# Moving the low parts of weights, rope, recurrence and gated sums from GpSimd to VectorE, and the high parts to ScalarE, in a two-layer hybrid attention block on one core

## Chip, cores and metric

The kernel runs on one core of one Trainium2 chip. The metric is the device time of one execution in microseconds (us), the median of three runs. A core has TensorE (PE in the rows, with its weight loads under PEld), VectorE (DVE), ScalarE (ACT), GpSimd (POOL) and SyncE (SP, which here issues the DMAs).

## The reference

Two layers over 512 latent tokens and 256 context tokens (768 together), model width 1024. Cut to what matters:

```python
for l in range(DEPTH):
    # adaLN: shift, scale and gate from w_mod; h = x * (1 + sc1) + sh1
    px, pc = split_in(h_x @ w_in), split_in(h_c @ w_in)
    y_mla  = attention of 8 heads, 64 + 32 (rope) wide, over ranks 256 and 128
    y_hg   = gated linear recurrence forwards and backwards, 4 heads of 128
             # f = lb + (1 - lb) * sigmoid(z); S = diag(f) S + k v^T; o = S^T q
    y_diff = (softmax(q1 k1) - lam * softmax(q2 k2)) v, 4 heads of 2 x 64, rope, RMS norm
    m  = sum over br of sigmoid(h @ w_gate[br] + b_gate[br]) * (y[br] @ w_branch[br])
    x  = layer_norm(alpha * x + g1 * (m @ w_o))
    x  = layer_norm(alpha * x + g2 * ((silu(gate) * up) @ w_ff2))   # gate, up = h @ w_ff1
```

Latent queries read context and latent tokens, context queries only context ones. All of it is float32.

## The kernel before

Every product is made from split operands: a high part (fp32r) and a low part (raw minus high), and three matmuls, high by high, high by low and low by high (`mm3`). A weight tile is loaded raw by a DMA (`wr`, 128x1024 or 128x512), `split_w` (L352) writes its high part `wh` and its low part `wl`, and both lie in rings of three buffers. `do_conv` (L365) splits tiles up to two jobs ahead of use.

All engines' orders are fixed when the program is built. A planner (`Clock`, L110) keeps a modelled clock for each engine, `self.ck.at[...]`, and every call goes through it. Its helper records every instruction, which is why all rows say L106 and work is told apart by tile names. Names: `h` activations (high and low), `wr`, `wh`, `wl` weights, `S` two score tiles of two PSUM banks each, `b` four single PSUM banks, `k` eight tiles for split heads, `s` slabs in SBUF, `sm` one-column statistics, `ident` the identity (a matmul with it is a transpose), `c` the conditioning vector, `ac` FFN activations, `colv` gate biases.

The program is two streams. One is a list of jobs, each of which uses one weight tile. The other is a generator for what waits on chains of small steps: `mla`, then `diff`, then `hgrn`, then the layer norm. `weave` (L433) puts them together. Where the generator yields `At(t)`, jobs are written until TensorE's modelled clock has reached t; where a job yields `Need(tok)`, the generator has to come that far first. The jobs of a layer come in this order: the projections (`uq_jobs`, `win_jobs`, and those of the modulation, `mod_block`), then `merge_jobs` for the branches 0, 2 and 1 (the first two numbers below are branch and place), then the output projection and the FFN (`sweep_jobs`). In `merge_jobs` a gate job multiplies `h` with a tile of `w_gate` and evacuates with a Sigmoid on ScalarE (`s<-b,colv` in the rows); a branch job multiplies the attention output with a tile of `w_branch`:

```python
                if len(st["y"]) < 4:
                    yield Need(f"y{l}_{br}")
                    yield Need(f"y{l}_2")
...
        lag = (6, 2, 8)[seq]
```

`y{l}_2` is set where `diff` ends. So the first branch job can be written only when `diff` is over; six gate jobs stand before it.

`diff` goes tile by tile (a head by 128 queries, against 768 keys for latent queries, 256 for context). Step by step: score matmuls into both `S` tiles (`sA`), a maximum on VectorE (`sm<-S`), an Exp on ScalarE (`s<-S,sm`), `sm<-sm,nlam,sm` and the difference `s<-s,sm,s` on VectorE (`sB3`), transposes of it (`b<-ident,s`, `S<-ident,s`) and their split into `k` (a cast on ScalarE, `k<-b,k` and `k<-S,k` on VectorE, `sC`), the product with the values (`b<-k,k`), and the norm of the output. In between `prep_qk` prepares the next head: rope, split, and value transposes. `hgrn` takes each head through log2 levels: on each level a copy `s<-k` on ScalarE, a matmul `S<-k,s`, and products of `k` tiles by gates (`k<-k,k`, `k<-k,s`); at L1427 one of them, 128x768, stands on GpSimd, the others on VectorE.

In the profiled execution the stages lie so, in us: start 0 to 120; layer 0: `mla` to 400, `diff` to 715, `hgrn` to 960, the rest of merge to 1080, norm and output projection to 1260, FFN to 1860; layer 1: `mla` to 2100, `diff` to 2275, `hgrn` to 2525, norm to 2660, FFN to 3000.

Of the kernel before, what the change touches and what calls it, by code (L numbers as in the profile page):

```python
# [10 lines left out]
F32 = mybir.dt.float32  # L11
# [221 lines left out]
class Job:  # L233
    def __init__(self, body, load=None, n=0, eng="vector", cost=0.0):
        self.body, self.load, self.n, self.eng, self.cost = body, load, n, eng, cost
        self.raw = self.hi = self.lo = None
        self.defer = self.late = False
        self.conv = None
        self.hold = False


class Kern:
# [647 lines left out]
    def uq_jobs(self, l):  # L890
# [4 lines left out]
        for half in range(2):  # L895
# [10 lines left out]
            def body(job, half=half):  # L906
# [3 lines left out]
                for hh in range(4):  # L910
# [3 lines left out]
                    def evac(ps, o, n):  # L914
                        if o == XO:
# [4 lines left out]
                            nc.gpsimd.tensor_tensor(qs[64:96, o:o + n], qs[64:96, o:o + n], tmp[64:96, :n], ALU.add)  # L920
# [49 lines left out]
    def win_jobs(self, l, names):  # L970
# [3 lines left out]
        for nmj, j in names:  # L974
# [18 lines left out]
            self.add(Job(body, self.load_fm(w, NK), 1024, "gpsimd", 24 * sum(mmcost(g[1]) for g in groups)))  # L993


    def mla(self, l):
# [54 lines left out]
        def sB2(i):  # L1051
# [5 lines left out]
            nc.gpsimd.tensor_scalar(pr[:, :n], pr[:, :n], rs[:], 1.0, ALU.mult, ALU.mult)  # L1057
# [85 lines left out]
    def diff(self, l):  # L1143
# [19 lines left out]
        def prep_qk(h):  # L1163
            rq, rqs, rk, rks, rv = st["raw", h]
            nc.gpsimd.tensor_tensor(rqs[:, XO:], rqs[:, XO:], rope[1][:, :TX], ALU.mult)
            yield
            nc.gpsimd.tensor_tensor(rks[:, XO:], rks[:, XO:], rope[1][:, :TX], ALU.mult)
            yield
            for rr, rs in ((rq, rqs), (rk, rks)):
                nc.vector.tensor_tensor(rr[:, XO:], rr[:, XO:], rope[0][:, :TX], ALU.mult)  # L1170
                nc.vector.tensor_tensor(rr[:, XO:], rr[:, XO:], rs[:, XO:], ALU.add)
                yield
# [14 lines left out]
            for g, m in ((0, 4), (4, 2)):  # L1187
                ps = self.bank()
# [5 lines left out]
                yield  # L1194
# [99 lines left out]
        for _ in prep_qk(0):  # L1294
            yield 1.0
        yield At(ck.ready(*[x[:, :, o0:] for x in st["qk", 0][:2]], st["v", 0]))
        n = len(tiles)
        per = n // 4
        pg = None
        for i in range(n + 3):  # L1300
            if i < n:
# [8 lines left out]
                if pg is not None:  # L1310
                    next(pg, None)
# [3 lines left out]
                if pg is not None:  # L1315
                    next(pg, None)
            elif i == n:
                sB3(i - 1)
            if 1 <= i <= n:
# [5 lines left out]
                if i < n and pg is not None:  # L1325
                    next(pg, None)
# [12 lines left out]
            if i < n and i % per == per - 1 and pg is not None:  # L1339
                for _ in pg:  # L1340
                    pass
# [8 lines left out]
    def hgrn(self, l):  # L1350
# [13 lines left out]
        def gen(h):  # L1364
            r = st.pop(("raw", h))
            KK, QQ, TT = self.k6([P, 2, T]), self.k6([P, 2, T]), self.k6([P, 2, T])
            for d, nmj in enumerate(("ff", "fb")):
                nc.scalar.activation(TT[:, d], r[nmj][:], AF.Sigmoid)
                nc.scalar.activation(KK[:, d], r[nmj][:], AF.Sigmoid, scale=-1.0)
                if l > 0:  # L1370
                    lb, l1 = self.lb[:, d, h:h + 1], self.lb1[:, d, h:h + 1]
                    nc.gpsimd.tensor_scalar(TT[:, d], TT[:, d], l1, lb, ALU.mult, ALU.add)
                    nc.gpsimd.tensor_scalar(KK[:, d], KK[:, d], l1, 1.0, ALU.mult, ALU.mult)
# [4 lines left out]
            nc.gpsimd.tensor_tensor(sq[:, o0:], KK[:, 0, o0:], KK[:, 1, o0:], ALU.add)  # L1378
# [5 lines left out]
            nc.gpsimd.tensor_tensor(g[:, o0:], g[:, o0:], sg[:, o0:], ALU.mult)  # L1384
# [28 lines left out]
            for lv in range(NLEV):  # L1413
# [13 lines left out]
                nc.gpsimd.tensor_tensor(kv, kv, tk, ALU.mult)  # L1427
# [105 lines left out]
    def merge_jobs(self, l, br, seq):  # L1533
# [30 lines left out]
        for o in range(8):  # L1564
# [9 lines left out]
            jg = Job(gate, self.load_fm(I["w_gate"][l, br][:, o * P:(o + 1) * P], NK), 1024, "gpsimd", 24 * sum(mmcost(g[1]) for g in groups))  # L1574
            gates.append(jg)

            def bran(job, o=o):
# [27 lines left out]
            brans.append(Job(bran, self.load_fm(I["w_branch"][l, br][:, o * P:(o + 1) * P], 4), 512, "gpsimd", 12 * sum(mmcost(g[1]) for g in groups)))  # L1605
# [8 lines left out]
    def sweep_jobs(self, key, w, nk, tiles, lhs, use_s, needs=(), keep=2):  # L1614
# [4 lines left out]
        for k in range(nk):  # L1619
# [31 lines left out]
            jb = Job(body, load, 1024, "vector")  # L1651
# [370 lines left out]
```

## Time and profile before

| | us |
|---|---|
| median of 3 runs (3018.76 to 3024.58) | 3023.1 |
| the profiled execution, its own time | 3024.47 |
| its span | 3022.7 |
| TensorE busy | 2764.9 |
| VectorE busy | 1652.6 |
| ScalarE busy | 1159.8 |
| GpSimd busy | 975.8 |

Busy times are sums over the instructions of an engine; engines work side by side, so they don't add up to the span. The span is what the profile covers, and the own time is that of the same execution as the runs are timed. The granted clock is TensorE's clock as the profile shows it, as a share of its full level (2.4 GHz); 0.5 is its lower level (1.2 GHz), and a mean in between is a mix of both.

### The profile page before, as it was taken

Reading aid. Unit: us, or ns where it says so; the run is one execution under the profiler, and the core shown is the slowest. Engines: PE = TensorE matmul, PEld = TensorE weight load, DVE = VectorE, ACT = ScalarE, POOL = GpSimd, SP = SyncE. Lnnn points to the kernel's source line nnn. Section 1 sums busy time; section 2 is a strip of 40 time slices with the busy share of each in tenths; the row PEclk is TensorE's granted clock in tenths of the full one; section 3 lists DMA queues with packets and bytes.
Section 4 is the critical chain, followed back from the end, with each engine's and each line's share of the span. In section 5 each row is a group of like instructions: output and inputs, shape, how many; then the busy total and the mean of one; then the engine's idle time right before and its main releaser. Section 6 shows DMA issues by size and latency. Waiting matters only on the chain. (4 is left out here: it accounts for less than half of the span.)

```text
span 3022.7 us, 39134 instructions
## 1 busy us (share of the span) xinstructions
PE 2764.9 (91%) x14899; PEld 2330.5 (77%) x14899; DVE 1652.6 (55%) x2410; ACT 1159.8 (38%) x2205; POOL 975.8 (32%) x685
## 2 busy tenths in 40 slices
PE   6999988878889998999999989999899899799997
PEld 3888867767778886788888768888787777688875
DVE  4555567667774137555543576455766764622235
ACT  4544435444432223443432355443544432322222
POOL 1343332223444433333320124344334654300002
PEclk8999999999999999999999999999999999899998
DMA  6433253323332444343533254324223444433331
GB/s 214 119 104 95 97 146 112 110 88 110 110 110 88 125 160 160 126 138 113 154 105 126 100 194 116 94 84 136 87 81 102 149 134 131 136 99 98 105 126 70
DMA packets 345523, 359.14 MB, mean 119 GB/s; under 512 B 31114, under 2 KB 263044, under 8 KB 345336
## 3 DMA queue, kind: packets, MB, share of 16 engines
q1 hardware_dynamic: 343144, 351.84, 37.1%
q10 hardware_dynamic: 1680, 4.42, 0.4%
q8 instruction: 117, 1.92, 0.3%
q14 instruction: 70, 0.57, 0.1%
q0 software_dynamic: 512, 0.39, 0.1%
HBM read 298.10 MB, written 58.49 MB: 118 GB/s over the span
## 5 line engine op out<-in xcount | busy, mean ns | idle before, releaser
L106 PE MATMUL b<-h,wh 128*128 128x512 f32 (+1 forms) x5152 | 1374.5, 355 | 35.0 <-ACT h L106 14.7
L106 PEld LDWEIGHTS b<-h,wh 128*128 128x128 f32 x5152 | 908.8, 193 | 164.4 <-ACT h L106 15.8
L106 PE MATMUL b<-h,wl 128*128 128x512 f32 (+1 forms) x2576 | 907.6, 352 | 0.8 <-DVE wl L106 0.8
L106 DVE TENSOR_TENSOR wl<-wr,wh 128x1024 fp32r<-128x1024 f32 (+1 forms) x250 | 357.6, 1433 | 472.1 <-ACT wh L106 469.9
L106 PEld LDWEIGHTS b<-h,wl 128*128 128x128 f32 x2576 | 494.7, 192 | 66.4 <-DVE wl L106 1.6
L106 ACT CAST wh<-wr 128x1024 fp32r<-128x1024 f32 (+1 forms) x304 | 301.0, 994 | 427.4 <-PE b L106 344.3
L106 POOL TENSOR_TENSOR sm<-sm,mhalf 128x1 f32<-128x1 f32 (+3 forms) x80 | 56.8, 711 | 1053.3 <-DVE sm L106 1041.2
L106 POOL TENSOR_TENSOR wl<-wr,wh 128x1024 fp32r<-128x1024 f32 (+1 forms) x134 | 292.1, 2180 | 228.2 <-ACT wh L106 176.6
L106 ACT ACTIVATE s<-S,sm 128x768 f32<-128x768 f32 (+1 forms) x170 | 135.3, 797 | 387.6 <-DVE sm L106 312.4
L106 POOL TENSOR_TENSOR ln<-ln,wr 128x512 f32<-128x512 f32 x84 | 119.5, 1424 | 222.6 <-issue 161.6
L106 PE MATMUL S<-wh,ac 128*128 128x512 f32 x512 | 175.0, 407 | 16.6 <-DVE ac L106 11.5
L106 DVE TENSOR_TENSOR k<-b,k 128x512 fp32r<-128x512 f32 (+1 forms) x136 | 85.3, 628 | 170.0 <-ACT k L106 169.7
L106 PE MATMUL b<-ident,s 128*128 128x128 f32 (+3 forms) x687 | 112.3, 278 | 70.3 <-DVE s L106 24.7
L106 PE MATMUL S<-k,s 128*128 128x128 f32 (+2 forms) x704 | 130.0, 309 | 35.7 <-DVE k L106 33.8
L106 PE MATMUL b<-k,wh 128*128 128x512 f32 (+1 forms) x576 | 160.0, 366 | 1.2 <-ACT wh L106 1.1
L106 DVE TENSOR_REDUCE sm<-S 128x1 f32<-128x768 f32 (+1 forms) x160 | 131.7, 838 | 52.9 <-PE S L106 52.8
L106 PEld LDWEIGHTS b<-ident,s 128*128 128x128 f32 (+3 forms) x687 | 80.3, 143 | 93.0 <-issue 27.7
L106 PE MATMUL S<-k,k 96*128 96x512 f32 (+2 forms) x576 | 136.9, 340 | 12.6 <-DVE k L106 10.4
L106 POOL TENSOR_SCALAR wh<-wr 128x1024 fp32r<-128x1024 f32 (+1 forms) x80 | 82.9, 1039 | 198.6 <-PE b L106 166.3
L106 PEld LDWEIGHTS S<-k,s 128*128 128x128 f32 x704 | 105.4, 203 | 50.0 <-issue 30.7
L106 DVE TENSOR_TENSOR k<-s,k 96x768 fp32r<-96x768 f32 (+7 forms) x92 | 116.3, 1281 | 47.3 <-ACT k L106 44.5
L106 POOL TENSOR_TENSOR s<-s,s 128x512 f32<-128x512 f32 (+2 forms) x88 | 114.3, 1309 | 66.1 <-DVE s L106 43.2
(184 smaller groups left out, 4210.9 us busy)
## 6 DMA issues: line engine op xcount, KB each, us to landing
wr<-in_w_ff_dram SPq DMA_DIRECT2D x154, 512.0 KB
wr<-in_w_mod_dram SPq DMA_DIRECT2D x96, 512.0 KB
d<-s SPq DMA_DIRECT2D x88, 384.0 KB
wr<-in_w_in_dram SPq DMA_DIRECT2D x64, 512.0 KB
s<-d SPq DMA_DIRECT2D x80, 384.0 KB
wr<-in_w_gate_dram SPq DMA_DIRECT2D x48, 512.0 KB
wr<-in_w_branch_dram SPq DMA_DIRECT2D x48, 256.0 KB
wr<-in_w_o_dram SPq DMA_DIRECT2D x24, 512.0 KB
```

Source lines behind the costliest of these rows:

```text
L106: return getattr(getattr(self.clock.nc, self.eng), op)(*a, **k)
```

## The change

GpSimd is taken out of the weight split, of `mla`'s normalisation, of rope, of the recurrence and of the gated sums. The high part of a weight is always written by ScalarE, the low part always by VectorE; the products and sums go to VectorE; two scalings of the gates in layer 1 go to ScalarE. In `diff`, the value transposes now yield an `At` for a free bank and for the loaded values, and the driving loop passes it on (`step`). The planner's choice between engines (`lo_eng`) goes away. GpSimd keeps the layer norm's affine, the modulation's part of it, and the power -0.5.

```diff
-    def split_w(self, hi, lo, raw, eng=None):
+    def split_w(self, hi, lo, raw):
         nc = self.nc
-        if self.kp is not None and not self.inhg and self.ck.at["gpsimd"] + 1.0 < self.ck.at["scalar"]:
-            nc.gpsimd.tensor_scalar(hi, raw, 1.0, 1.0, ALU.mult, ALU.mult)
-        else:
-            nc.scalar.copy(hi, raw)
-        (eng or nc.vector).tensor_tensor(lo, raw, hi.bitcast(F32), ALU.subtract)
-
-    def lo_eng(self, j):
-        if self.inhg and j.eng == "gpsimd" and self.ck.at["vector"] < self.ck.at["gpsimd"] + 1.0:
-            return self.nc.vector
-        return getattr(self.nc, j.eng)
+        nc.scalar.copy(hi, raw)
+        nc.vector.tensor_tensor(lo, raw, hi.bitcast(F32), ALU.subtract)
...
-            self.split_w(j.hi[:, :j.n], j.lo[:, :j.n], j.raw[:, :j.n], self.lo_eng(j))
+            self.split_w(j.hi[:, :j.n], j.lo[:, :j.n], j.raw[:, :j.n])
...
-            nc.gpsimd.tensor_scalar(pr[:, :n], pr[:, :n], rs[:], 1.0, ALU.mult, ALU.mult)
+            nc.vector.tensor_scalar(pr[:, :n], pr[:, :n], rs[:], None, ALU.mult)
...
-            nc.gpsimd.tensor_tensor(rqs[:, XO:], rqs[:, XO:], rope[1][:, :TX], ALU.mult)
-            yield
-            nc.gpsimd.tensor_tensor(rks[:, XO:], rks[:, XO:], rope[1][:, :TX], ALU.mult)
-            yield
             for rr, rs in ((rq, rqs), (rk, rks)):
+                nc.vector.tensor_tensor(rs[:, XO:], rs[:, XO:], rope[1][:, :TX], ALU.mult)
+                yield
...
             for g, m in ((0, 4), (4, 2)):
+                yield At(max(ck.next("b", 4), ck.ready(rv)))
                 ps = self.bank()
...
+        def step(pg):
+            r = next(pg, None) if pg is not None else None
+            if r is not None:
+                yield r
+                next(pg, None)
...
-                if pg is not None:
-                    next(pg, None)
+                yield from step(pg)
...
-                    nc.gpsimd.tensor_scalar(TT[:, d], TT[:, d], l1, lb, ALU.mult, ALU.add)
-                    nc.gpsimd.tensor_scalar(KK[:, d], KK[:, d], l1, 1.0, ALU.mult, ALU.mult)
+                    nc.scalar.activation(TT[:, d], TT[:, d], AF.Identity, scale=l1, bias=lb)
+                    nc.scalar.activation(KK[:, d], KK[:, d], AF.Identity, scale=l1)
...
-                nc.gpsimd.tensor_tensor(kv, kv, tk, ALU.mult)
+                nc.vector.tensor_tensor(kv, kv, tk, ALU.mult)
...
-                        nc.gpsimd.tensor_tensor(sg[:, oo:oo + n], sg[:, oo:oo + n], mo[:, oo:oo + n], ALU.add)
+                        nc.vector.tensor_tensor(sg[:, oo:oo + n], sg[:, oo:oo + n], mo[:, oo:oo + n], ALU.add)
```

Counted over the whole program, GpSimd goes from 690 instructions to 228, VectorE from 2412 to 2778, ScalarE from 1954 to 2074 (24 of these are table loads, which go from 13 to 37); TensorE and SyncE keep their numbers, 14369 and 916. What moves: 96 `wl` of 128x1024 and 38 of 128x512, 70 `wh` of 128x1024 and 10 of 128x512, 80 normalisations of `mla`, 88 rope products, `hgrn` products and gated sums (`s<-s,s`), 56 products of the recurrence, 8 sums `s<-k`, and 16 gate scalings.

Because the planner's clocks set the order, the change also moves instructions that it doesn't name. First, TensorE where layer 0's `diff` ends. Before, the transposes and the product of one of the last tiles are followed by matmuls of a gate job, `b<-h,wh` and `b<-h,wl`:

```order
L106 MATMUL b_6554<-ident,s_6437 128x128 x2
L106 MATMUL b_6559<-ident,s_6502 128x128
L106 MATMUL b_6559<-k_5776,k_6475 128x256 x12
L106 MATMUL b_6546<-h_114,wh_6277 128x256
L106 MATMUL b_6546<-h_115,wh_6277 128x256
L106 MATMUL b_6546<-h_114,wl_6278 128x256
```

After, the last tiles follow one upon the other, and the next row of a job is that of the first branch job, `b<-k,wh`:

```order
L106 MATMUL b_6876<-ident,s_6809 128x128 x2
L106 MATMUL b_6881<-ident,s_6846 128x128
L106 MATMUL b_6881<-k_6199,k_6819 128x256 x12
L106 MATMUL b_6912<-ident,s_6865 128x128 x2
L106 MATMUL b_6917<-ident,s_6896 128x128
L106 MATMUL b_6917<-k_6199,k_6875 128x256 x4
L106 MATMUL b_6933<-ident,s_6924 128x128
L106 MATMUL b_6933<-k_6199,k_6911 128x256 x4
L106 MATMUL b_6949<-ident,s_6940 128x128
L106 MATMUL b_6968<-s_6208,sel 2x512
L106 MATMUL b_6985<-k_6973,wh_6582 128x512 x2
L106 MATMUL b_6985<-k_6973,wl_6583 128x512
```

The last row of a job ahead of them is row 2938 and the next is row 2985: 46 rows (2939 to 2984) of four tiles and the end of two more stand with no job between them, where before gate jobs stand in every such place. In layer 1 the same is so for 23 rows (9657 to 9679), with one tile's scores. The same gate jobs now stand earlier in the program.

Second, ScalarE in the middle of layer 0's `diff`. Before, exps (`s<-S,sm`) of neighbouring tiles, with casts and the norm of the output between them:

```order
L106 ACTIVATE s_5349,sm_5352<-s_5349 128x128
L106 ACTIVATE s_5386,sm_5385<-S_3874,sm_5384 128x768
L106 ACTIVATE s_5395,sm_5394<-S_3875,sm_5393 128x768
L106 CAST wh_5439<-wr_5276 128x1024
L106 CAST k_5450<-b_5451 128x256
L106 ACTIVATE s_5180<-b_5457,subg_500 128x128
L106 ACTIVATE s_5464<-b_5457,sm_5298 128x128
L106 ACTIVATE s_5464,sm_5467<-s_5464 128x128
L106 ACTIVATE s_5485,sm_5484<-S_3874,sm_5483 128x768
L106 ACTIVATE s_5495,sm_5494<-S_3875,sm_5493 128x768
L106 COPY s_5438<-b_5443 128x512
```

After, at the same tiles, Sigmoids of gate jobs (`s<-b,colv`) stand among the exps, and a table load stands at each step from one to the other:

```order
L106 ACT_TABLE_LOAD
L106 ACTIVATE s_5803,sm_5802<-S_4129,sm_5801 128x768
L106 ACTIVATE s_5812,sm_5811<-S_4130,sm_5810 128x768
L106 CAST wh_5817<-wr_5600 128x1024
L106 ACT_TABLE_LOAD
L106 ACTIVATE s_5737<-b_5738,colv 128x512
L106 CAST k_5847<-b_5848 128x256
L106 ACTIVATE s_5589<-b_5854,subg_500 128x128
L106 ACTIVATE s_5861<-b_5854,sm_5699 128x128
L106 ACTIVATE s_5861,sm_5864<-s_5861 128x128
L106 ACT_TABLE_LOAD
L106 ACTIVATE s_5882,sm_5881<-S_4129,sm_5880 128x768
```

Of the 24 added loads 12 stand in layer 0's `diff` and 12 in layer 1's.

Third, the levels of the recurrence in layer 0's `hgrn`. Before, on VectorE:

```order
L106 TENSOR_TENSOR s_6893<-S_6886,ident 128x768
L106 TENSOR_TENSOR s_6895<-k_6808 128x768
L106 TENSOR_TENSOR k_6807<-k_6807,k_6808 128x384 x2
L106 COPY_PREDICATED s_6893<-mask,S_6898 128x768
L106 TENSOR_TENSOR k_6808<-s_6895 128x384
L106 TENSOR_TENSOR k_6807<-k_6807,s_6895 128x192x2 x2
L106 COPY_PREDICATED s_6893<-mask,S_6928 128x768
```

and beside it on GpSimd the wide product of each level:

```order
L106 TENSOR_TENSOR k_6806<-k_6806,k_6808 128x384x2
L106 TENSOR_TENSOR k_6806<-k_6806,s_6895 128x192x2x2
L106 TENSOR_TENSOR k_6806<-k_6806,k_6808 128x96x2x4
L106 TENSOR_TENSOR k_6806<-k_6806,s_6895 128x48x2x8
L106 TENSOR_TENSOR k_6806<-k_6806,k_6808 128x24x2x16
```

After, on VectorE alone:

```order
L106 TENSOR_TENSOR s_7078<-S_7071,ident 128x768
L106 TENSOR_TENSOR k_7022<-k_7022,k_7024 128x384x2
L106 TENSOR_TENSOR s_7080<-k_7024 128x768
L106 TENSOR_TENSOR k_7023<-k_7023,k_7024 128x384 x2
L106 COPY_PREDICATED s_7078<-mask,S_7093 128x768
L106 TENSOR_TENSOR k_7022<-k_7022,s_7080 128x192x2x2
L106 TENSOR_TENSOR k_7024<-s_7080 128x384
L106 TENSOR_TENSOR k_7023<-k_7023,s_7080 128x192x2 x2
```

The wide product `k<-k,k 128x384x2` (`128x192x2x2` on the next level) now stands on VectorE's queue ahead of the level's others.

## Rows read from the trace of the kernel before

**Rows 1.** The page, part 1: busy time and share of each engine.

```profile
PE 2764.9 (91%) x14899; PEld 2330.5 (77%) x14899; DVE 1652.6 (55%) x2410; ACT 1159.8 (38%) x2205; POOL 975.8 (32%) x685
```

**Rows 2.** Windows: stretch, its length, busy us of each engine; granted clock; DMA share.

```profile
120.00:400.00 280.00, 273.54 (x1697) 238.21 (x1696) 148.33 (x277) 127.73 (x282) 111.67 (x91) 1.00 0.40 122
400.00:625.00 225.00, 188.30 (x1069) 157.94 (x1067) 156.45 (x260) 101.92 (x229) 67.08 (x52) 0.92 0.34 106
625.00:715.00 90.00, 75.70 (x424) 64.09 (x425) 53.22 (x88) 52.01 (x105) 28.16 (x21) 0.92 0.35 111
715.00:960.00 245.00, 211.91 (x1337) 186.01 (x1336) 176.40 (x232) 81.02 (x155) 107.43 (x59) 0.95 0.30 101
1860.00:2100.00 240.00, 233.43 (x1412) 205.01 (x1411) 126.81 (x215) 99.70 (x211) 108.16 (x79) 1.00 0.37 111
2100.00:2275.00 175.00, 154.16 (x871) 132.30 (x870) 117.68 (x200) 86.33 (x196) 59.53 (x42) 0.95 0.33 99
2275.00:2525.00 250.00, 229.44 (x1234) 191.54 (x1233) 173.77 (x252) 93.87 (x182) 136.54 (x85) 0.99 0.38 118
2215.00:2275.00 60.00, 56.96 (x333) 49.65 (x332) 33.81 (x73) 31.31 (x74) 22.36 (x16) 0.97 0.31 94
```

**Rows 3.** Timeline, layer 1's diff: start, duration, idle before with its releaser in brackets.

```profile
2206.22 3.24 DVE L106 SCALAR_TENSOR_TENSOR s<-s,sm,s 128x768 f32<-128x768 f32 x1
2206.26 2.38 POOL L106 TENSOR_TENSOR wl<-wr,wh 128x1024 fp32r<-128x1024 f32 x1
...
2209.61 0.63 PE L106 MATMUL b<-ident,s 128*128 128x128 f32 x4 [1.71 <-DVE sm L106]
```

**Rows 4.** Timeline, layer 0's diff, a difference of two tiles with GpSimd still.

```profile
501.79 1.02 DVE L106 SCALAR_TENSOR_TENSOR s<-s,sm,s 128x768 f32<-128x768 f32 x1
```

**Rows 5.** Timeline, layer 0's hgrn, one level of the recurrence.

```profile
773.46 3.03 POOL L106 TENSOR_TENSOR k<-k,k 128x768 f32<-128x768 f32 x1 [1.47 <-ACT s L106]
...
776.52 0.94 ACT L106 COPY s<-k 128x768 f32<-128x768 f32 x1 [3.20 <-POOL k L106]
...
780.37 0.93 PE L106 MATMUL S<-k,s 128*128 128x128 f32 x4 [3.34 <-DVE k L106]
```

**Rows 6.** The page, part 5: groups (busy us, mean ns, idle before and its releaser).

```profile
L106 ACT CAST wh<-wr 128x1024 fp32r<-128x1024 f32 (+1 forms) x304 | 301.0, 994 | 427.4 <-PE b L106 344.3
L106 POOL TENSOR_TENSOR wl<-wr,wh 128x1024 fp32r<-128x1024 f32 (+1 forms) x134 | 292.1, 2180 | 228.2 <-ACT wh L106 176.6
```

**Rows 7.** Groups by form on VectorE, 2700 to 2940, FFN of layer 1.

```profile
L106 DVE TENSOR_TENSOR wl<-wr,wh 128x1024 fp32r<-128x1024 f32 x44 | 53.9, 1226 | 126.5 <-ACT wh L106 126.5
```

**Rows 8.** Groups by form on VectorE, 715 to 960, hgrn of layer 0.

```profile
L106 DVE TENSOR_TENSOR wl<-wr,wh 128x1024 fp32r<-128x1024 f32 x10 | 23.0, 2307 | 0.6 <-ACT wh L106 0.6
```

**Rows 9.** Groups by form on ScalarE, 400 to 715, diff of layer 0.

```profile
L106 ACT ACTIVATE s<-S,sm 128x768 f32<-128x768 f32 x32 | 28.9, 902 | 69.0 <-DVE sm L106 56.8 <-issue 12.0 <-ACT k L106 0.2
...
L106 ACT CAST k<-b 128x512 fp32r<-128x512 f32 x20 | 11.6, 582 | 3.3 <-PE b L106 3.3
...
L106 ACT ACT_TABLE_LOAD x7 | 9.0, 1283 | 0.1
```

**Rows 10.** Groups by form on VectorE, 400 to 715.

```profile
L106 DVE TENSOR_REDUCE sm<-S 128x1 f32<-128x768 f32 x32 | 29.2, 942 | 4.5 <-PE S L106 4.5
...
L106 DVE TENSOR_TENSOR k<-b,k 128x512 fp32r<-128x512 f32 x20 | 13.8, 690 | 22.6 <-ACT k L106 22.5
L106 DVE TENSOR_REDUCE sm<-S 128x1 f32<-128x256 f32 x16 | 6.0, 407 | 0.0
```

**Rows 11.** Timeline of ScalarE, 656 to 660: a table load among exps.

```profile
657.24 1.28 ACT L106 ACT_TABLE_LOAD   x1
658.54 0.69 ACT L106 ACTIVATE s<-b,colv 128x512 f32<-128x512 f32 x1
```

**Rows 12.** Timeline of TensorE, 636 to 682: its first and last waits behind loads.

```profile
639.01 0.33 PE L106 MATMUL b<-ident,s 128*128 128x128 f32 x1 [2.56 <-ACT s L106]
...
680.17 0.33 PE L106 MATMUL b<-ident,s 128*128 128x128 f32 x1 [2.00 <-ACT s L106]
```

More of the change, by code (lines that the diff above doesn't have):

```diff
@@ L233, with __init__ @@
 class Job:
-    def __init__(self, body, load=None, n=0, eng="vector", cost=0.0):
-        self.body, self.load, self.n, self.eng, self.cost = body, load, n, eng, cost
+    def __init__(self, body, load=None, n=0):
+        self.body, self.load, self.n = body, load, n
         self.raw = self.hi = self.lo = None
@@ L919, in evac @@
                             nc.vector.tensor_tensor(tmp[64:96, :n], ps[96:128, :n], self.rm[96:128], ALU.mult)
-                            nc.gpsimd.tensor_tensor(qs[64:96, o:o + n], qs[64:96, o:o + n], tmp[64:96, :n], ALU.add)
+                            nc.vector.tensor_tensor(qs[64:96, o:o + n], qs[64:96, o:o + n], tmp[64:96, :n], ALU.add)
                         else:
@@ L992, in body @@
                 self.done.add(f"win{l}_{nmj}{j}")
-            self.add(Job(body, self.load_fm(w, NK), 1024, "gpsimd", 24 * sum(mmcost(g[1]) for g in groups)))
+            self.add(Job(body, self.load_fm(w, NK), 1024))
     def mla(self, l):
@@ L1193, in prep_qk @@
                 nc.vector.tensor_tensor(v2[:, g:g + m, P:], pv, v2[:, g:g + m, 0:P].bitcast(F32), ALU.subtract)
-                yield
+                if g == 0:
+                    yield
             st["v", h] = v2
@@ L1293, in diff @@
         yield At(ck.ready(*[r[:, o0:] for r in st["raw", 0]], *rope))
-        for _ in prep_qk(0):
-            yield 1.0
+        for r in prep_qk(0):
+            yield r or 1.0
         yield At(ck.ready(*[x[:, :, o0:] for x in st["qk", 0][:2]], st["v", 0]))
+        def step(pg):
[3 more added lines that the diff above has]
+                next(pg, None)
         n = len(tiles)
@@ L1314, in diff @@
                 sB(i, 1)
-                if pg is not None:
-                    next(pg, None)
+                yield from step(pg)
             elif i == n:
@@ L1324, in diff @@
                     pg = prep_qk(h + 1)
-                if i < n and pg is not None:
-                    next(pg, None)
+                yield from step(pg)
             if i >= 2:
@@ L1339, in diff @@
             if i < n and i % per == per - 1 and pg is not None:
-                for _ in pg:
-                    pass
+                for r in pg:
+                    if r is not None:
+                        yield r
                 pg = None
@@ L1377, in gen @@
             nc.vector.scalar_tensor_tensor(q[:, o0:], q[:, o0:], HG_SCALE, sq[:, o0:], ALU.mult, ALU.mult)
-            nc.gpsimd.tensor_tensor(sq[:, o0:], KK[:, 0, o0:], KK[:, 1, o0:], ALU.add)
+            nc.vector.tensor_tensor(sq[:, o0:], KK[:, 0, o0:], KK[:, 1, o0:], ALU.add)
             nc.vector.tensor_tensor(QQ[:, 0, o0:], q[:, o0:], TT[:, 1, o0:], ALU.mult)
@@ L1383, in gen @@
             nc.scalar.activation(sg[:, o0:], g[:, o0:], AF.Sigmoid)
-            nc.gpsimd.tensor_tensor(g[:, o0:], g[:, o0:], sg[:, o0:], ALU.mult)
+            nc.vector.tensor_tensor(g[:, o0:], g[:, o0:], sg[:, o0:], ALU.mult)
             vt = self.slab()
@@ L1573, in gate @@
                     yield c
-            jg = Job(gate, self.load_fm(I["w_gate"][l, br][:, o * P:(o + 1) * P], NK), 1024, "gpsimd", 24 * sum(mmcost(g[1]) for g in groups))
+            jg = Job(gate, self.load_fm(I["w_gate"][l, br][:, o * P:(o + 1) * P], NK), 1024)
             gates.append(jg)
@@ L1604, in bran @@
                     self.done.add(f"m{l}_{seq}")
-            brans.append(Job(bran, self.load_fm(I["w_branch"][l, br][:, o * P:(o + 1) * P], 4), 512, "gpsimd", 12 * sum(mmcost(g[1]) for g in groups)))
+            brans.append(Job(bran, self.load_fm(I["w_branch"][l, br][:, o * P:(o + 1) * P], 4), 512))
         lag = (6, 2, 8)[seq]
@@ L1650, in body @@
                 held.clear()
-            jb = Job(body, load, 1024, "vector")
+            jb = Job(body, load, 1024)
             jb.late = k >= 3
```

## The prediction

> **What bounds the kernel now.** I read the busy times first, then windows by stage, then the timeline around TensorE's waits. TensorE is busy 2764.9 of 3022.7 us [rows 1], so what can be won is its idle time, some 258 us, and time at its lower clock. The windows say where it lies [rows 2]: in layer 0's `mla` TensorE idles 280.00 − 273.54 = 6.5 us, in `diff` 36.7 + 14.3 = 51.0, in `hgrn` 33.1; in layer 1's `mla` 6.6, `diff` 20.8, `hgrn` 20.6. The six stretches of 120 to 960 and 1860 to 2525 together hold 125.5 us. The granted clock in them is 0.92, 0.92, 0.95, 0.95 and 0.99 in `diff` and `hgrn`, and 1.00 in both `mla` stretches. A mean of 0.92 is 16% of the time at 1.2 GHz: twice (1 − clock) by the length gives 36.0 + 14.4 + 24.5 + 17.5 + 5.0 = 97 us at that level.
>
> Why TensorE waits there is to be seen in two places. In `diff`, the difference `s<-s,sm,s` takes 3.24 us on VectorE while GpSimd writes a low part `wl` beside it for 2.38; TensorE's transposes stand behind it and have idled 1.71 us when they start [rows 3]. The same instruction, of the same shape, takes 1.02 us when GpSimd is still [rows 4]. In `hgrn`, GpSimd's `k<-k,k` takes 3.03 us, the copy on ScalarE has idled 3.20 for it, and the level's matmuls have idled 3.34 for a product on VectorE [rows 5]. Weights show it by means: VectorE's `wl` of 128x1024 takes 1226 ns in layer 1's FFN [rows 7] and 2307 ns in `hgrn`, where GpSimd works [rows 8]; GpSimd's own `wl` has a mean of 2180 [rows 6]. So an instruction of VectorE that reads two operands from SBUF is stretched two- or threefold beside GpSimd's work, and these stretched instructions stand on the chain that TensorE waits for. The reductions, which read PSUM, keep 942 ns [rows 10].
>
> The page "SBUF — State Buffer" of the Trainium skill, section "SBUF: two separate sides", has a cause for this: VectorE and GpSimd share a pair of ports, held by one whole instruction at a time, which a VectorE instruction with two SBUF inputs needs. The trace agrees with 3.24 against 1.02 us.
>
> **What the change gives.** GpSimd loses the work beside these chains. `diff` and `hgrn` (560 us in layer 0, 425 in layer 1) hold 125.5 − 13.0 = 112.4 us of the idle time. How much would be left has two bounds. In a piece of `diff` in which, as it happens, no instruction of VectorE is stretched, 2215 to 2275, TensorE idles 3.04 of 60.00 us, 5.1%, at a clock of 0.97 [rows 2]: 50 us of 985, so 62 go. In the `mla` stretches, the same weave of chains and jobs, it idles 13.0 of 520, 2.5%: 25 us of 985, so 88 go. I choose the middle, 75. At a clock of 0.97, 6% of 985 us is at the lower level, 59 in place of 97 us; the 38 us less are 87% busy (859.5 of 985), and work at half speed takes twice as long, so 38 × 0.87 / 2 = 16 us. Gains: 75 + 16 = 91 us.
>
> **What it costs.** There are four terms.
>
> VectorE and ScalarE get more work. VectorE takes 366 instructions: 96 `wl` × 1.23 = 118 us, 38 half ones × 0.62 = 24, 56 products of the recurrence × 1.02 = 57, and the other 176 at a value between 0.29 and 1.02, I take 0.63, so 111: 310 us in all [rows 4, 7]. It loses the stretch. Of its present 1652.6 us [rows 1] nothing is on the path outside these stretches, and in them it is busy 53 to 72% [rows 2]. ScalarE takes 80 casts × 0.99, 79 us [rows 6], 16 small scalings and the table loads. I cost that at nothing in `diff` and `hgrn`, where the 5.1% was read with both engines about half busy (33.8 and 31.3 of 60.0 us); if that cover is gone the idle goes back toward what it is. In `mla`, TensorE is busy 98% because nothing is late; 80 normalisations and all of its low parts on VectorE make it later: +5 us, between 0 and the present 13 once more.
>
> Table loads go from 13 to 37. One takes 1283 ns and ScalarE starts the next instruction at its end (657.24 + 1.28, next 658.54) [rows 9, 11]. In the last part of layer 0's `diff` there are 7 of them; behind four of them TensorE idles, 2.56 us the first time and 2.00 the last, 7.45 in all [rows 12]. That is 1.06 per load. 24 × 1.06 = 25 us. Bounds: 0, if the chain has slack at every one, and 24 × 2.00 = 48.
>
> The Trainium skill speaks against this change here: "ScalarE: Activation LUTs", section "What ACT_TABLE_LOAD costs", gives 1283 ns for the load, which the trace shows, and about 1380 ns of drain with it, 2.66 us a switch. The next instruction starting at the load's end shows no drain behind it in this trace; by the page's price the term would be 64 us instead of 25.
>
> The job list runs dry where `diff` ends. Because the gate jobs now stand earlier, 46 rows of TensorE in layer 0 and 23 in layer 1 follow one upon the other with no job between them, and TensorE waits for each step of each tile. One tile with 768 keys, without cover, is at least two reductions 2 × 0.94, two exps 2 × 0.90, the difference 1.02, the cast 0.58, the subtraction 0.69 and the transposes 0.63 [rows 3, 4, 9, 10]: 6.6 us; with the small statistics and the norm of the output between them I take 8, and 6 for a tile of context. The most it can be is the pace of now, with jobs in between: 32 long reductions and 16 short ones are 16 + 8 tiles in 315 us, 13 us each [rows 10]. Layer 0's rows hold two long tiles, two short ones and the end of the pipeline: 8 + 8 + 6 + 6 + 7 = 35 us, in which I count 11 us of TensorE's own work, so 24 us lost. Layer 1's hold one tile and the end: 19.5 − 7.7 = 12. Together 36 us (6.8 periods of a long tile, less 19): 26 with the lower bound, 69 with the upper. That is new idle time: the gate jobs have done their work elsewhere, where they filled what would be filled by others.
>
> The value transposes that now wait for a bank: 0. What stands behind the waiting transposes on TensorE is the next job, and the `At` puts jobs ahead of them instead; the next head's values are wanted a whole tile later. It can give up to 10 us, five of the waits of 2 us seen in `diff`, and I take none. The other stages (start, merge's rest, norms, FFN) already have `wl` on VectorE or nothing of the change on their path: 0. DMAs and their queue keep their number.
>
> Sum: 5 + 25 + 36 = 66 us of costs against 91 us of gains, 25 us less than the profiled execution's 3024.47: **2999 us**. The median of the runs shown is 1.4 us lower, which is inside their spread.
>
> **The rivals.**
> - *Each load costs what TensorE idled at the last one.* 24 × 2.00 = 48 in place of 25: 3022 us, no change that can be told. For it: 2.00 is seen [rows 12]. Against: three of seven loads show no idle behind them.
> - *Each load costs as much as the worst.* 24 × 2.56 = 61: 2999 + 36 = 3035, slower. In the middle of `diff` ScalarE also casts the high parts, so a load stands in a fuller queue than those seen. This is also the side on which the page's price lies.
> - *The bare ends decide (slower).* If a tile without cover takes the 13 us that it takes now, the ends cost 6.8 × 13 − 19 = 69 us in place of 36 and the kernel takes 3032; it gets slower from 91 − 30 = 61 us, that is from 11.8 us a tile. For it: each step waits for the one before across three engines, and a TensorE that idles drops to its lower clock, as the 0.92 shows. Against: the steps' own times add up to 6.6.
> - *GpSimd isn't the cause.* The waits were VectorE's queue; the products that leave GpSimd are then done one after the other on VectorE, whose level of the recurrence holds one 128x768 more, about 1.02 us by its unstretched time. Half the gain, 45 us less: 3044, slower. Against: 3.24 and 1.02 for one instruction.
>
> **How the numbers follow.** The forecast has 0.62, with 2960 to 3016 as its own range: lower if loads are hidden (25) and the idle left is that of `mla` (13), higher by 13 if it is that of the unstretched piece, and a little more from `mla`. No change, 3022: 0.09. The worst load, 3035: 0.06; the bare ends, 3032: 0.13; half the gain, 3044: 0.10. A difference of 0.2%, 6 us, is about what a measurement of this kernel can tell from no change. So faster 0.62, same 0.09, slower 0.29. The range goes down to 2950, where the loads cost nothing, the idle left is least and the ends are cheap (25 + 13 + 10 less), and up to 3048 to hold the last of the rivals.
>
> **What would show it right or wrong** in the profile of the changed kernel: the mean of `s<-s,sm,s` at about 1.0 us and of `wl` at about 1.23 in every stage; GpSimd's busy time under 350 us; TensorE's idle share in `diff` and `hgrn` near 5% outside of the ends; 37 table loads, with some 1.1 us of idle behind each; two stretches at the end of `diff` with 24 and 12 us of idle and a lower clock. The prediction is wrong if `diff`'s idle stays at 12 to 16% with GpSimd still (then the cause is another), if tiles in the bare ends are 12 us apart, or if VectorE becomes over 90% busy in `hgrn`.

## The result and the profile after

The changed kernel takes 2989.3 us in the median (2987.5 to 2991.8, four runs) against 3022.1 of the kernel before (3018.8 to 3024.6) beside it: a ratio of 0.9893, interval 0.9876 to 0.9910. That is 33 us less; 25 had been forecast. Each set of runs below stands beside its own runs of the kernel before, so kernels are compared by their ratios; 0.1% is 3 us.

The page after, part 1, answers to [rows 1]:

```profile
span 2985.4 us, 38612 instructions
PE 2751.4 (92%) x14899; PEld 2327.0 (78%) x14899; DVE 1726.1 (58%) x2776; ACT 1278.0 (43%) x2325; POOL 274.6 (9%) x223
```

GpSimd's busy time falls from 975.8 to 274.6 us, VectorE's rises only from 1652.6 to 1726.1 with 366 instructions more. Over the whole program TensorE's busy time falls by 13.5 us (2764.9 to 2751.4) for the same 14899 matmuls.

Two groups on VectorE in 400 to 800, where `diff` lies, with the columns of [rows 9], in the kernel before:

```profile
L106 DVE SCALAR_TENSOR_TENSOR s<-s,sm,s 128x768 f32<-128x768 f32 x16 | 26.8, 1672 | 0.6
...
L106 DVE TENSOR_SCALAR s<-s,sm 128x128 f32<-128x128 f32 x24 | 14.4, 600 | 18.6 <-POOL sm L106 18.6
```

and in the changed kernel, with two groups of its `hgrn` (730 to 955), the recurrence's wide product and the low parts:

```profile
L106 DVE SCALAR_TENSOR_TENSOR s<-s,sm,s 128x768 f32<-128x768 f32 x16 | 16.3, 1019 | 0.6
...
L106 DVE TENSOR_SCALAR s<-s,sm 128x128 f32<-128x128 f32 x24 | 6.9, 287 | 17.5 <-POOL sm L106 17.5
```

```profile
L106 DVE TENSOR_TENSOR k<-k,k 128x768 f32<-128x768 f32 x16 | 18.0, 1124 | 0.0
L106 DVE TENSOR_TENSOR wl<-wr,wh 128x1024 fp32r<-128x1024 f32 x11 | 13.4, 1218 | 0.0
```

The difference has a mean of 1019 ns in place of 1672, and 1.02 us is what it takes with GpSimd still [rows 4]; the 3.24 of [rows 3] was one of the longest. `wl` is back at 1218 in `hgrn` [rows 8: 2307], and the wide product has a mean of 1124 where the one shown on GpSimd took 3.03 us [rows 5].

Jobs move between stages when the planner's clocks change, so stages are compared whole: the mixers (`mla` to the end of merge), and what lies between. Windows of the kernel before (columns as in [rows 2]):

```profile
120.00:1103.00 983.00, 892.46 (x5348) 772.09 (x5347) 556.67 (x886) 391.82 (x814) 384.26 (x274) 0.96 0.36 112
1103.00:1861.00 758.00, 711.21 (x3633) 596.04 (x3632) 428.21 (x507) 298.55 (x491) 202.09 (x130) 0.97 0.42 134
1861.00:2563.00 702.00, 650.61 (x3653) 554.23 (x3651) 428.61 (x683) 290.41 (x604) 324.09 (x222) 0.98 0.37 113
2563.00:3022.00 459.00, 418.15 (x1856) 344.44 (x1856) 187.22 (x198) 122.74 (x165) 44.90 (x30) 0.96 0.33 107
```

and of the changed kernel from landmark to landmark:

```profile
122.00:1068.00 946.00, 878.63 (x5328) 761.76 (x5327) 599.78 (x1088) 450.15 (x873) 18.34 (x28) 0.97 0.37 116
1068.00:1820.00 752.00, 710.62 (x3637) 596.81 (x3636) 424.57 (x510) 296.54 (x489) 188.63 (x122) 0.97 0.42 135
1820.00:2529.00 709.00, 653.43 (x3651) 560.38 (x3650) 464.19 (x839) 350.49 (x665) 12.74 (x20) 0.96 0.37 113
2529.00:2985.00 456.00, 416.91 (x1856) 343.53 (x1855) 184.52 (x200) 122.85 (x165) 42.48 (x28) 0.96 0.33 108
```

Layer 0's mixers went from 983 to 946 us: idle from 90.5 to 67.4, busy 13.8 less. Layer 1's went from 702 to 709: idle from 51.4 to 55.6, and the granted clock fell from 0.98 to 0.96. Of the two mixers only layer 0's gained, 37 us, and layer 1's gave 7 back. The other stages took 9 us less (758 to 752, 459 to 456), and the start 2 more.

Inside layer 0's mixers, the idle time of `diff` did not fall. Before, `diff` and what follows it to the end of merge:

```profile
420.00:692.00 272.00, 230.17 (x1316) 194.38 (x1315) 180.94 (x322) 129.55 (x296) 77.31 (x63) 0.93 0.33 101
692.00:1103.00 411.00, 375.98 (x2285) 329.41 (x2285) 214.47 (x277) 126.62 (x225) 187.50 (x117) 0.97 0.35 113
```

and of the changed kernel the `diff` of both layers without its end:

```profile
449.00:688.00 239.00, 212.01 (x1241) 180.30 (x1240) 147.56 (x294) 150.83 (x291) 9.78 (x18) 0.96 0.35 111
2081.00:2255.00 174.00, 157.02 (x881) 134.06 (x880) 112.58 (x209) 108.46 (x213) 6.52 (x12) 0.98 0.32 98
```

Layer 0's `diff` idled 41.8 of 272 us before (15%). Now it idles 27.0 of 239 (11%) up to its end, and 22.1 more in the end, as the next windows show. What follows it went from 35.0 us of idle time to 6.8 (730 to 1068, the row stands below): that is where layer 0's gain of idle time lies.

The two costs that were foreseen are there. The ends of `diff`, as windows in layer 0 and layer 1:

```profile
688.00:730.00 42.00, 19.88 (x84) 15.48 (x84) 18.05 (x50) 15.19 (x49) 3.25 (x6) 0.63 0.06 21
2255.00:2281.00 26.00, 13.13 (x58) 11.44 (x56) 9.24 (x25) 8.42 (x23) 2.17 (x4) 0.58 0.01 3
```

TensorE idles 42.0 − 19.9 = 22.1 us and 26.0 − 13.1 = 12.9 at clocks of 0.63 and 0.58. The timeline of TensorE in the first of them:

```profile
694.52 1.12 PE L106 MATMUL b<-ident,s 128*128 128x128 f32 x4 [1.30 <-DVE s L106]
...
703.90 1.09 PE L106 MATMUL b<-ident,s 128*128 128x128 f32 x4 [3.73 <-DVE sm L106]
...
711.93 0.52 PE L106 MATMUL b<-ident,s 128*128 128x128 f32 x3 [2.82 <-DVE sm L106]
...
718.22 0.88 PE L106 MATMUL b<-ident,s 128*128 128x128 f32 x3 [3.67 <-DVE sm L106]
...
722.76 0.45 PE L106 MATMUL b<-ident,s 128*128 128x128 f32 x1 [2.82 <-DVE s L106]
726.83 0.45 PE L106 MATMUL b<-ident,s 128*128 128x128 f32 x1 [2.76 <-DVE s L106]
730.46 0.80 PE L106 MATMUL b<-k,wh 128*128 128x512 f32 x1 [1.40 <-ACT k L106]
```

From one tile's transposes to the next it is 9.4, 8.0 and 6.3 us, and each step starts behind VectorE. Table loads, as a group of ScalarE over the program, and one of them with the Sigmoid behind it:

```profile
L106 ACT ACT_TABLE_LOAD x37 | 47.5, 1283 | 1.4 <-PEq L2006 0.7
```

```profile
573.00 1.28 ACT L106 ACT_TABLE_LOAD   x1
574.30 0.69 ACT L106 ACTIVATE s<-b,colv 128x512 f32<-128x512 f32 x1
```

TensorE's transposes behind that one had idled 2.02 us:

```profile
575.04 0.33 PE L106 MATMUL b<-ident,s 128*128 128x128 f32 x1 [2.02 <-ACT s L106]
```

### The profile page after: what moved, and what is told of

Its sections match the earlier page's. It is cut to its first block, busy times and chain, and to the rows that moved or that the text cites. A ratio compares the mean times of both kernels' runs of the same rounds, so it can differ in the third digit from the quotient of the medians.

```text
span 2985.4 us, 38612 instructions
## 1 busy us (share of the span) xinstructions
PE 2751.4 (92%) x14899; PEld 2327.0 (78%) x14899; DVE 1726.1 (58%) x2776; ACT 1278.0 (43%) x2325; POOL 274.6 (9%) x223
## 5 line engine op out<-in xcount | busy, mean ns | idle before, releaser
L106 DVE TENSOR_TENSOR wl<-wr,wh 128x1024 fp32r<-128x1024 f32 (+1 forms) x384 | 475.1, 1244 | 581.1 <-ACT wh L106 580.2
L106 ACT CAST wh<-wr 128x1024 fp32r<-128x1024 f32 (+1 forms) x384 | 379.3, 995 | 403.9 <-PE b L106 321.6
L106 PEld LDWEIGHTS S<-wh,ac 128*128 128x128 f32 x512 | 97.9, 193 | 43.1 <-DVE ac L106 15.4
L106 PEld LDWEIGHTS S<-k,k 96*128 96x128 f32 (+1 forms) x576 | 101.4, 192 | 38.6 <-DVE k L106 23.1
L106 PEld LDWEIGHTS b<-k,wh 128*128 128x128 f32 x576 | 103.4, 195 | 29.8 <-ACT k L106 11.0
L106 ACT ACTIVATE wr<-wr,cact 128x512 f32<-128x512 f32 x84 | 59.9, 723 | 142.1 <-DVE ln L106 115.8
L106 ACT COPY s<-b 128x512 f32<-128x512 f32 (+4 forms) x160 | 79.2, 505 | 82.6 <-PE b L106 79.0
```

Of the source, the lines that this page charges most:

```text
L106: return getattr(getattr(self.clock.nc, self.eng), op)(*a, **k)
```

## The experiments

**Is it GpSimd's work beside VectorE?** Idle work was put back on GpSimd, on a scratch tile that nobody reads. The planner doesn't see it, so the other engines' orders stay row by row:

```diff
+        if self.kp is not None:
+            g, d = self.nc.nc.gpsimd, self.idle
+            g.tensor_scalar(d[:, :1], hi.bitcast(F32)[:, :1], 0.0, None, ALU.mult)
+            for _ in range(4):
+                g.tensor_tensor(d[:], d[:], d[:], ALU.mult)    # e_write: g.memset(d[:], 0.0)
```

> The changed kernel with idle work on GpSimd: after each of the 193 weight splits of the mixer stages, GpSimd waits for the high part, reads one column of it, and multiplies a 128x256 scratch tile by itself four times. Nobody waits for the result; the orders of TensorE, VectorE, ScalarE and SyncE are those of the changed kernel, row by row. If GpSimd's work beside VectorE is the cause (my theory), the stretch comes back: s<-s,sm,s means above 1.5 us, wl above 1.6 in the mixers, and the time rises from 2989 by 30 to 90 us. If the waits were GpSimd's own place on the chain (rival: it was slow, and VectorE waited for its results), nothing waits here and the time stays within 6 us of 2989.

> The same as e_read, but the four idle instructions are memsets of the scratch tile: GpSimd writes SBUF and reads nothing, but for the one column. The Trainium skill's page SBUF - State Buffer (SBUF: two separate sides) says that a VectorE instruction with two SBUF inputs contends only with a GpSimd instruction that reads SBUF; by that the time stays within 10 us of the changed kernel's 2989 and s<-s,sm,s near 1.05 us. If any work of GpSimd stretches VectorE, this run lies where e_read lies.

With products, the time is 3072.9 us, ratio 1.0168 (1.0153 to 1.0183), 83 us over the changed kernel; with memsets 2989.7, ratio 0.9893 (0.9879 to 0.9908), no change. But the two don't occupy GpSimd alike: a product takes 0.82 us, a memset 0.32. And my expectation overlooked that something does wait for GpSimd: the power -0.5 in the norm of `diff` stands in its queue behind the idle work. So the memsets were made ten, which is as long as four products.

> As e_write with ten memsets per split in place of four, so that GpSimd is about as long occupied at each split (10 x 0.32 us) as by e_read's four products (4 x 0.81 us). If e_read's 84 us came from VectorE being held by reads, this run stays within 6 us of 2989. If they came from GpSimd's queue, in which the power -0.5 that diff waits for stands behind the idle work, this run lies above 3040 as e_read does. In between, both have a share, and this run measures the queue's.

3041.2 us, ratio 1.0056 (1.0035 to 1.0078): 49 us over the changed kernel, in between. The queue has a large share. The groups on VectorE in 400 to 800 show it by the wait for the power. With products:

```profile
L106 DVE TENSOR_SCALAR s<-s,sm 128x128 f32<-128x128 f32 x24 | 6.9, 286 | 45.9 <-POOL sm L106 45.9
```

with ten memsets:

```profile
L106 DVE TENSOR_SCALAR s<-s,sm 128x128 f32<-128x128 f32 x24 | 6.9, 286 | 55.6 <-POOL sm L106 55.6
```

The wait of 17.5 us grows to 45.9 and 55.6. In the kernel before it was 18.6, by the same group, so this queue hardly played a part in the change itself; it spoilt the experiment as a measure. The last pair takes the wait away. In the norms of `diff`, and likewise in those of `hgrn`, a reciprocal on VectorE stands where the power stood, so these norms are scaled by another value:

```diff
-            nc.gpsimd.tensor_tensor(rs[:], ss[:], self.mhalf[:, 0:1], ALU.pow)
+            nc.note("gpsimd", "tensor_tensor", (rs[:], ss[:], self.mhalf[:, 0:1], ALU.pow), {})
+            nc.nc.vector.reciprocal(rs[:], ss[:])
```

> The changed kernel without GpSimd's power in the norms of diff and hgrn: VectorE takes a reciprocal there in place of the power -0.5, so those norms are scaled by 1/x. Nothing in the mixers waits for GpSimd any more. It is the base for e_readr: 2975 to 2992, the wait for the power (17.5 us of VectorE's idle time in layer 0's diff) being partly on the path.

> e_rec with the idle products of e_read on GpSimd. In e_read and e_write10b VectorE waited 45.9 and 55.6 us for the power that stood behind the idle work, against 17.5 in the changed kernel; e_write10b's 52 us more for 38 of such wait make some 38 of e_read's 84 us. Here nothing waits for GpSimd. If the rest is VectorE held by reads: 46 us over e_rec, between 30 and 60, with VectorE's busy time some 85 us higher. If all of e_read's 84 us were the queue: within 6 us of e_rec.

The base takes 2969.1 us, ratio 0.9834 (0.9820 to 0.9849), lower than I expected; with the idle products it is 3022.3, ratio 1.0014 (1.0005 to 1.0024): 1.80%, 54 us, from work for which next to nobody waits. What is left is a wait of ScalarE's casts, since the idle work reads a column of the high part; over the whole run, by the waits of ScalarE (us in total, times, longest us):

```profile
ACT wh L106 <- POOL idle L362: 3.1, 1, 3.1
ACT wh L106 <- POOL idle L360: 0.3, 1, 0.3
```

Two groups of VectorE, first the base, then with the products:

```profile
L106 DVE SCALAR_TENSOR_TENSOR s<-s,sm,s 128x768 f32<-128x768 f32 x16 | 16.3, 1019 | 0.6
L106 DVE TENSOR_TENSOR s<-s,s 128x512 f32<-128x512 f32 x24 | 16.3, 685 | 0.5 <-DMA s<-d 0.2
```

```profile
L106 DVE SCALAR_TENSOR_TENSOR s<-s,sm,s 128x768 f32<-128x768 f32 x16 | 19.4, 1211 | 0.6
L106 DVE TENSOR_TENSOR s<-s,s 128x512 f32<-128x512 f32 x24 | 19.1, 801 | 0.4
```

1019 to 1211 ns, 685 to 801; VectorE's busy time goes from 1735.9 to 1828.6 us by the pages, 93 us in all. The reductions, which read PSUM, stay at 944 and 941. The idle work costs time in layer 1's mixers too, 726 us with the products against 700 in the base:

```profile
1812.00:2512.00 700.00, 649.69 (x3639) 557.13 (x3639) 466.40 (x858) 346.40 (x660) 0.00 (x0) 0.97 0.37 113
1837.00:2563.00 726.00, 660.20 (x3651) 560.32 (x3649) 513.62 (x860) 349.54 (x665) 314.06 (x386) 0.96 0.36 110
```

The theory stands: GpSimd's work beside VectorE costs time. The rival by which it harms nobody who doesn't wait for it is out. How much of the change's 33 us comes that way is another question.

**Which part of the change carries it?** The weight split alone, and all but the weight split:

```diff
# e_weights, in the kernel before
-        if self.kp is not None and not self.inhg and self.ck.at["gpsimd"] + 1.0 < self.ck.at["scalar"]:
-            nc.gpsimd.tensor_scalar(hi, raw, 1.0, 1.0, ALU.mult, ALU.mult)
-        else:
-            nc.scalar.copy(hi, raw)
-        (eng or nc.vector).tensor_tensor(lo, raw, hi.bitcast(F32), ALU.subtract)
+        nc.scalar.copy(hi, raw)
+        nc.vector.tensor_tensor(lo, raw, hi.bitcast(F32), ALU.subtract)
# e_rest, in the changed kernel: split_w and lo_eng as before
```

> The kernel before with the weight split alone changed: high parts always on ScalarE, low parts always on VectorE; all else stays on GpSimd. By its order no bare end stands in either layer, and 31 table loads. If GpSimd's work beside VectorE is the cause, the splits are 375 of its 701 us less, so it gives half or more of the 33 us: 2995 to 3005. If the other parts (recurrence, normalisation, gated sums) carried the gain: within 6 us of 3022.

> The changed kernel with the weight split as before (GpSimd takes high and low parts by the planner's choice); recurrence, normalisation, rope, sums and the bank wait as changed. No bare end by its order, 27 table loads. Half of the gain or less by my theory, since GpSimd keeps 375 us or more of reads: 3000 to 3015. If GpSimd's own place on the chains (recurrence, normalisation) was what cost the time, nearly all of it: 2985 to 2995.

3000.9 us, ratio 0.9935 (0.9921 to 0.9950), and 2994.7, ratio 0.9919 (0.9901 to 0.9936): 20 and 24 us less, where both together give 32. Neither carries it alone, and each alone gives more than half. That they add up to more than the whole is not settled; the whole has 37 table loads where these have 31 and 27, which is 4 and 6 us by the next experiment, and e_rest holds the value transposes' wait for a bank as well. The difference in `diff` (400 to 715) tells the two apart, first with the splits moved, then with the splits left on GpSimd:

```profile
L106 DVE SCALAR_TENSOR_TENSOR s<-s,sm,s 128x768 f32<-128x768 f32 x16 | 16.3, 1018 | 0.6
L106 DVE SCALAR_TENSOR_TENSOR s<-s,sm,s 128x768 f32<-128x768 f32 x16 | 20.8, 1301 | 0.6
```

The recurrence tells them apart the other way. TensorE's waits for VectorE's `k` in 690 to 970, where layer 0's `hgrn` lies (us in total, times, longest us), in the kernel before, in e_weights, in e_rest and in the changed kernel:

```profile
PE S L106 <- DVE k L106: 25.4, 13, 4.9
PE S L106 <- DVE k L106: 25.2, 13, 5.6
PE S L106 <- DVE k L106: 4.0, 6, 1.1
PE S L106 <- DVE k L106: 3.5, 1, 3.5
```

These waits stay when the splits alone leave GpSimd, and go when the recurrence's products leave it. The changed kernel's one wait of 3.5 us still belongs to the end of `diff`. So behind `diff` layer 0 won most of its idle time by the recurrence's own move, and e_weights won its 20 us elsewhere. It didn't win them by having the low parts sooner: TensorE had waited for GpSimd's low parts only 2.0 us in the whole of the kernel before. `e_rest` still came out better than I expected from 375 us of splits on GpSimd. By windows, layer 0's mixers take 956 us (124 to 1080) and 951 (124 to 1075), layer 1's 703 in both, against 702 before: neither won anything in layer 1.

**What do the loads cost?** The gates without their Sigmoid:

```diff
-                    nc.scalar.activation(sg[:, oo:oo + n], ps[:, :n], AF.Sigmoid, bias=...)
+                    nc.scalar.activation(sg[:, oo:oo + n], ps[:, :n], AF.Identity, bias=...)
```

> The changed kernel with Identity in place of Sigmoid in the gates' evacuation, so the gates are left without their sigmoid; table loads go from 37 to 7 and all other rows stay. My term of 24 loads at 1.06 us expects 25 us less, 2964; if the loads are hidden, within 6 us of 2989; at 2.0 us each, 2941.

2972.0 us, ratio 0.9831 (0.9809 to 0.9852), 0.62% or 19 us less for 30 loads: 0.62 us each.

**What do the bare ends cost?**

```diff
-        lag = (6, 2, 8)[seq]
+        lag = (7, 2, 8)[seq]
```

> The changed kernel with seven gate jobs in place of six ahead of the first branch job (lag 7, 2, 8). By its order the bare rows at the end of layer 0's diff go from 46 to 21 and layer 1's are gone; table loads go from 37 to 41. My term of 36 us for the bare ends, of which some 9 would stay in layer 0, expects 27 less and 4 more for the loads: 2966. If the idle time only moves elsewhere, because gate jobs that fill the end are missing later, within 6 us of 2989.

2988.3 us, ratio 0.9887 (0.9873 to 0.9902): nothing, with 41 table loads in place of 37, which is 2 us by the price above. My expected 27 us fail here. The windows say why. The changed kernel's `diff` and what follows it to the end of merge:

```profile
449.00:730.00 281.00, 231.89 (x1325) 195.78 (x1324) 165.61 (x343) 166.02 (x338) 13.03 (x24) 0.91 0.31 97
730.00:1068.00 338.00, 331.18 (x2084) 294.09 (x2085) 223.33 (x368) 121.91 (x214) 5.31 (x4) 0.99 0.39 126
```

the same with seven gate jobs:

```profile
450.00:733.00 283.00, 238.38 (x1378) 201.95 (x1376) 167.57 (x346) 174.36 (x347) 12.99 (x24) 0.92 0.31 98
733.00:1071.00 338.00, 325.61 (x2038) 288.31 (x2038) 222.42 (x367) 118.75 (x209) 5.31 (x4) 0.98 0.38 125
```

The seventh job brings 6.5 us of work into `diff` (231.9 to 238.4 busy), and its idle falls from 49.1 to 44.6; from there on the busy time falls by 5.6 and the idle rises by as much (6.8 to 12.4). The first stretch is 2 us longer than it was, the second as long. The work that fills a hole in `diff` is missing in what follows, and leaves a hole of the same size there.

**Both removed, with the whole computation.** The first branch's gates are evacuated by Identity, and their Sigmoid is taken when the branch job begins, after `diff`:

```diff
+                if seq == 0:
+                    nc.scalar.activation(sg[:, o0:], sg[:, o0:], AF.Sigmoid)
                 if seq > 0:
                     mo = self.slab()
```

> The changed kernel with seven gate jobs ahead of the first branch job, and the first branch's gates evacuated by Identity, with their Sigmoid taken by ScalarE when the branch job begins: the whole computation, 7 table loads, bare rows 21 and 0. From e_noload (17 us less) and e_lag7 (1 less): 2971, if the Sigmoids taken later are hidden beside the branch jobs; up to 2985 if TensorE's evacuation waits for each of them.

> The changed kernel with late Sigmoids as in e_late7, but six gate jobs ahead of the first branch job, so the bare ends are as changed. If the seventh job gives nothing, as beside the table loads: 2966 to 2972, as e_late7. If the bare ends cost what I priced once the loads are gone: 2985 or more.

With seven gate jobs 2966.3 us, ratio 0.9824 (0.9810 to 0.9839); with six 2969.8, ratio 0.9825 (0.9806 to 0.9843). Both are 0.7%, 21 us, better than the changed kernel and 53 better than the kernel before, and the seventh job gives nothing without the loads too. Windows of the first, both mixers:

```profile
123.00:1052.00 929.00, 868.10 (x5312) 752.08 (x5311) 598.82 (x1087) 432.13 (x863) 18.34 (x28) 0.98 0.37 118
1806.00:2504.00 698.00, 648.74 (x3652) 557.16 (x3651) 463.72 (x839) 338.82 (x661) 12.75 (x20) 0.98 0.37 114
```

929 and 698 us: layer 0's mixers lose 17 us more, layer 1's 11. With six gate jobs, layer 0's `diff` up to its end:

```profile
446.00:679.00 233.00, 209.40 (x1251) 178.00 (x1250) 152.36 (x300) 132.41 (x283) 9.78 (x18) 0.98 0.36 115
```

**The value transposes' wait for a bank** taken out of the changed kernel:

```diff
             for g, m in ((0, 4), (4, 2)):
-                yield At(max(ck.next("b", 4), ck.ready(rv)))
                 ps = self.bank()
...
-                if g == 0:
-                    yield
+                yield
```

> The changed kernel without the value transposes' wait for a bank in the planner: prep_qk yields where it did before. My term for it was 0, with up to 10 us to be gained by it: 2989 to 2999; if the transposes' wait costs more than it gives (it puts jobs ahead of them that are then missing at the end of diff), below 2983.

2998.6 us, ratio 0.9922 (0.9902 to 0.9943): the wait gives 0.29%, 9 us, just at what can be told; the two intervals overlap by a little. This kernel also has 39 table loads in place of 37, about 1 us by the price above.

## Why the prediction was right, by its steps

The sign was right and the time lies in the forecast's own range. The stretch went as foreseen, but the idle time was not won where it was priced, and the sum came near the result partly by luck. By its steps:

- *VectorE's instructions are stretched by GpSimd's, and TensorE waits behind them.* Shown, by the means after the change, by 20 us from the splits alone in e_weights and by 54 us from idle products in e_readr. GpSimd's own slowness on the chains is another thing; e_rest, which takes the recurrence, the normalisation and the sums from GpSimd but leaves it the splits, won 24 us, and TensorE's waits in `hgrn` went with the recurrence's products. Whether by their stretch of VectorE or by their own length, no run here parts for the recurrence.
- *Some 5% of idle time left in `diff` and `hgrn`.* In `diff`, outside of the ends, 11% is left in layer 0 and 10% in layer 1 (27.0 of 239 and 17.0 of 174 us). That is near the 12 to 16% by which the prediction wanted to be called wrong. The added loads are not the reason: in e_late, which has none of them, 23.6 of 233 us are left, 10%. So the stretch was a part of `diff`'s idle time, 15% before, and what holds the rest is open. What follows `diff` idles 6.8 of 338 us in layer 0, 2%, and 17.2 of 248 in layer 1 (2281 to 2529), 7%.
- *Gains of 75 us of idle time.* The working has a slip: 125.5 us is the idle time of `diff` and `hgrn` alone (36.7 + 14.3 + 33.1 + 20.8 + 20.6), so `mla`'s 13.0 was taken off a second time. Put right, the bounds are 76 and 101 us, their middle 88, and the forecast is 13 us lower, 2986. Net of the costs the idle time of both mixers fell from 141.9 to 122.9, 19 us. With 15 for the loads, 7 for `mla`, 9 from the bank wait and nothing for the ends, as below, an estimate of what was won is 19 + 15 + 7 − 9 = 32 us, less than half of the term.
- *16 us from the clock.* The mean clock didn't rise as forecast: layer 0's mixers went from 0.96 to 0.97, layer 1's from 0.98 to 0.96, and part of the lower level now lies in the bare ends (0.63 and 0.58). But the term stands for TensorE's busy time, and that fell by 13.8 us in layer 0's mixers and rose by 2.8 in layer 1's, 11 us net.
- *Loads, 25 us.* 15 for the 24 added ones by e_noload's 0.62 a load, in place of 1.06, which was read from the last part of `diff` alone. By the Trainium skill's 2.66 us a switch ("ScalarE: Activation LUTs", section "What ACT_TABLE_LOAD costs") it would be 80 us for e_noload's 30 loads, which gave 19 when they went. Some of a load can lie in idle time of ScalarE, but the trace shows no drain behind it either: the next instruction starts 20 ns after the load's end.
- *Bare ends, 24 + 12 us.* The idle there is 22.1 and 12.9 us, and a tile takes 9.4 us in place of 8. The size was right, the meaning wrong: it isn't a cost of its own. With a seventh job there the time stays, because the same work is missing later.
- *`mla`, 5 us.* 11.4 and 8.5 us of idle by its windows (122 to 449 and 1820 to 2081: 327.0 − 315.6 and 261.0 − 252.5) against 13.0, 7 more, in longer stretches.
- *The bank wait, 0.* A gain of 9 us, near the 10 I allowed.
- *All other stages, 0.* 7 us less in the profile, which no run here explains.

So the sum hit with errors on both sides: the gain of idle time some 40 us too high, the clock 5, against costs too high by 36 for the ends and 10 for the loads, and 16 us of gains that were put at nothing (the bank wait and the other stages). Of the rivals, the half gain with GpSimd not the cause forecast a slower kernel and is out as a whole by e_readr; in the recurrence it is open. Why layer 1's mixers stay between 698 and 709 us in every kernel without idle work on GpSimd whose windows were read (702 before) is open too; TensorE is busy for 648 to 653 us of them.

## What to carry to other kernels

An engine that hardly anybody waits for can still cost time: compare the mean of one form of instruction with and without its neighbour at work before you count an offload as free. To price a hole in TensorE's work, ask where the work comes from that would fill it; if that place waits for a chain too, filling moves the hole. Keep two functions of different tables apart in the order where a planner that doesn't know of the loads weaves them; here a Sigmoid moved behind `diff` gave 21 us.

## What the runs showed of the hardware

Ten memsets or four products occupied GpSimd alike, but only work that reads SBUF stretched VectorE: e_write10b's VectorE was busy 1728.0 us by its page, as the changed kernel's 1726.1, and its difference stayed at 1019 ns; e_read's was busy 1814.4 us. The Trainium skill's "SBUF — State Buffer", section "SBUF: two separate sides", says just this of VectorE instructions with two SBUF inputs, and the runs agree. The stretch here was 0.12 to 0.19 us an instruction on the mean with products of 0.82 us, and 2.2 us with a low part of 2.38 [rows 3].

The wait for GpSimd's power, a 128x1 instruction of 0.54 us, was worth more than I would have thought: with a reciprocal on VectorE in its place the kernel took 0.59%, 18 us, less.
